# A two-block network on one core: one set of durations for the merge of threads, and a delta layer whose convolutions take their taps from PSUM

## The chip, the cores and the metric

One core of one Trainium2 chip runs the whole program in one launch. The time is the device time of that launch in microseconds (us); several runs are taken, and their median is the time of a kernel. TensorE does the matmuls (PE in the profile, its weight loads PEld), VectorE is DVE, ScalarE is ACT, GpSimd is POOL; SyncE (SP) issues the loads of weights. PSUM is the memory that matmuls write, SBUF the one that all other operands lie in.

## The reference, cut to what matters

Two blocks of a network in float32 on one sequence: 256 rows of width 1024, ahead of which the first block puts 16 rows of "meta" tokens (272 rows in the kernel). The first block has two layers: a gated delta layer and an mLSTM, each followed by a feed-forward part with a short convolution. The second block is a swiglu, three mixers side by side (spatial gating, latent attention, memory attention) under gates, and a second swiglu. The change touches the delta layer's projection and convolution:

```python
proj = h @ w_in
qkv = jax.nn.silu(causal_depthwise_conv(proj[..., :o1], conv_w)).astype(f32)
z = proj[..., o1:o2].astype(f32).reshape(B, L, GDN_V_HEADS, GDN_HEAD_DIM)
...
a_mat = jnp.eye(CHUNK, dtype=f32) + jnp.einsum('bhnid,bhnjd->bhnij', kb, kc) * decay * strict
rhs = jnp.concatenate([vc * bc[..., None], kb * jnp.exp(G)[..., None]], -1)
sol = lax.linalg.triangular_solve(a_mat, rhs, left_side=True, lower=True)
...
o = rms_norm(o, norm_w) * jax.nn.silu(z)
return o.reshape(B, L, GDN_VAL_DIM).astype(h.dtype) @ w_out
```

q and k have 1024 columns each, v and z 2048 each; the convolution has 4 taps along the rows for each of the 4096 columns of q, k and v.

## The kernel before, in words

**Products.** Activations lie with features on the partitions and the 272 rows along the free axis. A float32 product is made of three matmuls, since operands are split into a high part and the rest: `linear_g` (L398) runs for each of 8 blocks of 128 input features k, and for each feature tile of 128 output columns, wh x xh, wh x xl and wl x xh, all into one PSUM bank of the tile (`ps`). So a feature tile is 24 matmuls of 128x272. `wload` (L357) brings 512 KB of weights by one DMA on SP's queue (`wraw`), ACT copies them to `wh`, and wl = wraw - wh is formed by POOL in two pieces of 128x512 in the delta layer, elsewhere mostly by DVE. Buffers for wraw, wh and wl: three each.

**The delta layer** (20 to 368 us of the span; `gdn`, L1316). Several coroutines share the engines. `projections` runs `gdn_proj` for four groups of heads g (each 2 blocks of 256 columns of k and q and 2 of v, so 8 feature tiles) and puts the 8 blocks of z (`gdn_z`) wherever a group may not begin yet: group 2 begins when group 0's work ahead of the recurrence is done, group 3 after group 1's. `before`, in two lanes (first and second 128 rows), transposes and norms q and k (`kqp`, `kqT`), forms the decayed products (`kk`, `dp`, BA) and inverts the triangular matrix by blocks: level by level, a matmul `yp` (RT x Br), ACT's copy of it (Y), the matmuls `w`, and DVE's write of the new blocks into RT, which the next `yp` needs; `zp`, Z and `r2p` end it with a correction. A core coroutine runs the recurrence (`up`, `vs`, `sp`, `op`), `after` the norm of the output (`on`, `otp`, the root `rq_a`). The last 16 rows of all heads are a last small chunk, the tail (`gdn_tail_pre` and what follows it); `rsp`, `r`, `zs`, `og` lead from it to project_out (`ps<-og`, first at 368.32 us).

A block of the projection of q, k or v: two loads of 128x4x256 (four k each), for each load 12 matmuls on either feature tile, so that the two banks of the pool "pq" are both in use and end 12 matmuls apart. Then `conv4` (L974) for each: ACT copies PSUM to SBUF (`cx`), ACT scales PSUM by the last tap (`cy`), DVE adds the three other taps from cx, shifted by 1, 2 and 3 rows, ACT takes tanh of the half (`cth`), and DVE or (from feature tile 14 on, so all 16 of v and two of k) POOL makes the silu in one or two operations.

**What sets the order.** PE's order is written by `Threads` (L97 on, its loop `run`). Coroutines yield lists of what their next matmuls need: tiles, tags of banks or numbers. The planner keeps a clock for PE and lists of busy times for ACT, DVE and POOL ("A", "V", "G"), fills them by `COST` (a fixed part and one for each column), scaled by `KC`; `LAG`, `SAME` and `PLAG` are the handover from another engine, on the same engine, and to PE. It resumes the coroutine whose needs are met first. The order within DVE, ACT and POOL is made by the scheduler of the language from the program in that order. So another set of durations gives another order of the same matmuls.

Of the kernel before, what the change touches and what calls it, by code (L numbers as in the profile page):

```python
# [8 lines left out]
F32 = mybir.dt.float32  # L9
# [5 lines left out]
ALU = mybir.AluOpType  # L15
# [6 lines left out]
T = S + NM  # L22
KD = D // 128
# [73 lines left out]
class Threads:  # L97
# [4 lines left out]
    LAG, SAME, PLAG = 0.25, 0.13, 0.6  # L102
    KC = 1.0
    COST = {"PE": (0.0, 1 / 2400), "A": (0.06, 0.00085), "V": (0.07, 0.00104), "G": (0.1, 0.0022)}
# [29 lines left out]
    def note(self, key, outs, ins, n, ahead=False):  # L134
        a, b = self.COST[key]
        t = max([self.ready(x, key) for x in ins], default=0.0)
        if key == "PE":
            t = self.clk["PE"] = max(t, self.clk["PE"]) + a + b * n
        else:
            t = self.place(key, self.clk["PE"] if ahead else t, (a + b * n) * self.KC)  # L140
        for x in ins:
            self.read[x.tensor.name] = max(t, self.read.get(x.tensor.name, 0.0))
        for o in outs:
            self.rdy[o.tensor.name] = (0.0, key) if ahead else (t, key)
# [64 lines left out]
class Kern:  # L209
    def __init__(self, ctx, tc, ins, out):  # L210
# [20 lines left out]
        self.lane = None  # L231
        self.ordered = False
# [47 lines left out]
    def ps(self, shape=(128, T), name="ps"):  # L280
        return self.pp.tile(list(shape), F32, tag="pp", name=name)
# [536 lines left out]
    def embed(self):  # L818
# [3 lines left out]
        f = self.xt  # L822
# [3 lines left out]
        w = self.i["gdn_w_in"][0]  # L826
# [7 lines left out]
        with self.tc.manual_schedule(engines={mybir.EngineType.DVE}):  # L834
# [24 lines left out]
            low = {1: prefetch(0, KD, 6144, 32), 3: prefetch(0, 4, 1024, 256), 6: prefetch(4, 4, 1024, 256)}  # L859
# [114 lines left out]
    def conv4(self, ps, ct, out):  # L974
# [3 lines left out]
        x = self.p_l.tile([128, T], F32, tag="cx", name="cx", bufs=3)  # L978
        self.A.copy(x[:], ps)
        self.act(y[:], ps, AF.Copy, scale=w(3))  # L980
        for s in (1, 2, 3):
            self.stt(y[:, s:], x[:, :T - s], w(3 - s), y[:, s:], ALU.mult, ALU.add)
# [8 lines left out]
    def gdn_proj(self, X, g):  # L991
        W = self.i["gdn_w_in"][0]
        qs, ks, v0, v1 = (self.vslot() for _ in range(4))
        for base, dst in ((1024 + g * 256, ks), (g * 256, qs), (2048 + g * 512, v0), (2304 + g * 512, v1)):
            yield from self.linear_g(W, base, 256, KD, X, T, lambda m, p: self.conv4(p, base // 128 + m, dst[:, m, :]))
# [710 lines left out]
    def first(self):  # L1706

        i = self.i
        X = self.embed()
        self.th.KC, self.th.LAG, self.th.SAME, self.th.PLAG = 0.8, 0.25, 0.18, 0.65  # L1710
        Y = yield from self.gdn(X)
        self.th.KC, self.th.LAG, self.th.SAME, self.th.PLAG = 0.9, 0.25, 0.13, 0.6
# [68 lines left out]
        self.th.KC, self.th.LAG, self.th.SAME, self.th.PLAG = 0.9, 0.3, 0.13, 0.7  # L1781
# [666 lines left out]
```

## Time and profile before

| | us |
|---|---|
| median of 3 runs | 1668.43 |
| lowest and highest | 1667.3, 1671.02 |
| the profiled execution, its own time | 1671.11 |
| its span | 1669.3 |
| mean granted clock of TensorE | 0.973 |

The profile is of one execution. Rows of it are groups of instructions by line, engine, operation and tile (out<-in); since a helper records every operation, nearly all have line L190, and one goes by tiles. "Idle before" is time in which the engine did nothing ahead of these instructions, and what ended it. The chain of waits follows the end of the program (or of a stretch) back through what released each step. PE's records of matmuls overlap, so that a matmul's price is read from the distance of starts.

### The profile page before, as it was taken

Reading aid. Unit: us, or ns where it says so; the run is one execution under the profiler, and the core shown is the slowest. Engines: PE = TensorE matmul, PEld = TensorE weight load, DVE = VectorE, ACT = ScalarE, POOL = GpSimd, SP = SyncE. Lnnn points to the kernel's source line nnn. Section 1 sums busy time; section 2 is a strip of 40 time slices with the busy share of each in tenths; the row PEclk is TensorE's granted clock in tenths of the full one; section 3 lists DMA queues with packets and bytes.
Section 4 is the critical chain, followed back from the end, with each engine's and each line's share of the span. In section 5 each row is a group of like instructions: output and inputs, shape, how many; then the busy total and the mean of one; then the engine's idle time right before and its main releaser. Section 6 shows DMA issues by size and latency. Waiting matters only on the chain.

```text
span 1669.3 us, 31255 instructions
## 1 busy us (share of the span) xinstructions
PE 1564.4 (94%) x11980; PEld 1475.4 (88%) x11980; DVE 1120.0 (67%) x2223; ACT 927.9 (56%) x1877; POOL 579.2 (35%) x535
## 2 busy tenths in 40 slices
PE   8889888899999998999899998999997899999999
PEld 6788778799899997888899998999985789999987
DVE  5788877766888757457877668464659663566643
ACT  4567767655566554446566556454553655564542
POOL 3574555320200002550344441122275548511221
PEclk9799999999999999999999999999998999999999
DMA  5331221226355554335366564566553335656564
GB/s 158 89 89 52 69 64 47 77 90 214 106 178 174 169 175 111 96 115 164 107 185 192 175 185 148 163 199 192 173 166 111 111 93 150 183 164 188 180 189 151
DMA packets 239100, 235.39 MB, mean 141 GB/s; under 512 B 11511, under 2 KB 226407, under 8 KB 238951
## 3 DMA queue, kind: packets, MB, share of 16 engines
q1 hardware_dynamic: 238326, 231.86, 46.4%
q8 instruction: 94, 1.54, 0.4%
q0 software_dynamic: 496, 1.41, 0.4%
q14 instruction: 56, 0.45, 0.1%
q10 hardware_dynamic: 128, 0.13, 0.0%
HBM read 232.32 MB, written 1.05 MB: 140 GB/s over the span
## 4 chain that ended last, share of the span: by engine, by line
PE 68%; DVE 22%; ACT 5%; DMA 3%; issue 2%; POOL 0%; ACTq 0%; POOLq 0%; DVEq 0%
PE ps L190 52%; PE pst L190 5%; DVE cy L190 3%; DVE rq_a L190 3%; ACT wh L190 2%; DVE RT L190 2%; DVE wl L190 1%; DVE rq_y L190 1%; PE memp L190 1%; DMA wraw<-in_ffn_w_up_dram 1%; DVE xn L190 1%; PE rsp L190 1%; DVE on L190 1%; PE w L190 1%; PE up L190 1%
## 5 line engine op out<-in xcount | busy, mean ns | idle before, releaser
L190 PE MATMUL ps<-xhl,wh 128*128 128x256 f32 (+2 forms) x4496 | 861.6, 294 | 28.9 <-DVE py L190 11.1
L190 PEld LDWEIGHTS ps<-xhl,wh 128*128 128x128 f32 x4496 | 703.0, 193 | 38.3 <-DVE py L190 6.9
L190 ACT CAST wh<-wraw 128x1024 fp32r<-128x1024 f32 (+2 forms) x436 | 448.0, 1029 | 389.8 <-PE ps L190 255.9
L190 PE MATMUL ps<-xhl,wl 128*128 128x256 f32 (+2 forms) x2248 | 626.0, 287 | 0.8 <-DVE wl L190 0.8
L383 POOL TENSOR_TENSOR wl<-wraw,wh 128x512 fp32r<-128x512 f32 (+3 forms) x264 | 334.7, 1291 | 658.2 <-ACT wh L190 622.8
L190 PEld LDWEIGHTS ps<-xhl,wl 128*128 128x128 f32 x2248 | 423.9, 192 | 1.0 <-DVE wl L190 1.0
L190 DVE TENSOR_TENSOR wl<-wraw,wh 128x1024 fp32r<-128x1024 f32 (+2 forms) x237 | 287.4, 1213 | 182.4 <-ACT wh L190 179.2
L190 POOL TENSOR_TENSOR wl<-wraw,wh 128x512 fp32r<-128x512 f32 x134 | 173.9, 1319 | 153.1 <-ACT wh L190 136.2
L190 PE MATMUL ps<-hh,wh 128*128 128x256 f32 (+1 forms) x1056 | 191.1, 283 | 0.0
L190 PEld LDWEIGHTS ps<-hh,wh 128*128 128x128 f32 x1056 | 163.2, 189 | 0.0
L190 PE MATMUL ps<-hh,wl 128*128 128x256 f32 (+1 forms) x528 | 149.7, 284 | 0.0
L190 DVE SCALAR_TENSOR_TENSOR fy<-ps,pvt,fy 128x256 f32<-128x256 f32 (+2 forms) x176 | 84.9, 488 | 25.1 <-ACT fy L190 23.2
L190 PEld LDWEIGHTS ps<-hh,wl 128*128 128x128 f32 x528 | 99.4, 188 | 0.0
L190 DVE SCALAR_TENSOR_TENSOR cy<-cx,pvt,cy 128x271 f32<-128x271 f32 (+2 forms) x96 | 74.5, 779 | 13.5 <-ACT cy L190 12.5
L190 DVE TENSOR_TENSOR hh<-fy,hh 128x256 fp32r<-128x256 f32 (+1 forms) x88 | 64.4, 735 | 13.2 <-ACT hh L190 12.8
L190 POOL MEMSET mvt<- 128x4 f32 x4 | 0.4, 102 | 176.0 <-PE ps L190 176.0
L190 ACT ACTIVATE fy<-ps,pvt 128x272 f32<-128x272 f32 (+1 forms) x88 | 49.5, 568 | 12.3 <-PE ps L190 11.8
L190 DVE TENSOR_TENSOR py<-ps,rstd 128x256 f32<-128x256 f32 x72 | 29.9, 420 | 37.9 <-PE ps L190 37.9
L190 PE MATMUL pst<-wh,hh 128*128 128x512 f32 x176 | 55.1, 394 | 0.0
L190 ACT CAST hh<-fy 128x256 fp32r<-128x256 f32 (+1 forms) x88 | 35.7, 407 | 29.8 <-DVE fy L190 29.0
L190 DVE CAST_PREDICATED RT<-lvl,w 128x512 f16<-128x512 uint8 x67 | 44.9, 683 | 7.1 <-PE w L190 6.8
L190 PE MATMUL ps<-og,wh 128*128 128x272 f32 x256 | 48.6, 289 | 0.1
(523 smaller groups left out, 2420.4 us busy)
## 6 DMA issues: line engine op xcount, KB each, us to landing
wraw<-in_ffn_w_up_dram SPq DMA_DIRECT2D x88, 512.0 KB
wraw<-in_ffn_w_gu_dram SPq DMA_DIRECT2D x88, 512.0 KB
wraw<-in_ffn_w_down_dram SPq DMA_DIRECT2D x79, 512.0 KB
wraw<-in_gdn_w_in_dram SPq DMA_DIRECT2D x48, 512.0 KB
wraw<-in_w_in_dram SPq DMA_DIRECT2D x41, 512.0 KB
wraw<-in_ml_w_in_dram SPq DMA_DIRECT2D x24, 512.0 KB
wraw<-in_gdn_w_out_dram SPq DMA_DIRECT2D x16, 512.0 KB
wraw<-in_ml_w_out_dram SPq DMA_DIRECT2D x8, 512.0 KB
```

The source lines that it names most:

```text
L190: r = f(*args, **kw)
L383: eng.tensor_tensor(l[:, a, b], r[:, a, b], h[:, a, b].bitcast(F32), ALU.subtract)
```

## The change

Three things. The planner's durations become one set for the whole program, and `KC` goes; the settings that the delta layer, the stages after it and the mixers had are taken out. `conv4` loses the copy cx: the three taps read the PSUM bank itself. `gdn_proj` goes by feature tile: one load of 128x8x128 holds all eight k of one tile, a tile takes one bank, and before it starts the planner is told to wait for the last reader of the tile two back (`free`).

```diff
--- before.py
+++ after.py
@@ -99,9 +99,8 @@
 
 
 
-    LAG, SAME, PLAG = 0.25, 0.13, 0.6
-    KC = 1.0
-    COST = {"PE": (0.0, 1 / 2400), "A": (0.06, 0.00085), "V": (0.07, 0.00104), "G": (0.1, 0.0022)}
+    LAG, SAME, PLAG = 0.25, 0.05, 0.6
+    COST = {"PE": (0.006, 0.000441), "A": (0.19, 0.00084), "V": (0.155, 0.00104), "G": (0.1, 0.0025)}
 
     def __init__(self):
         self.clk = {"PE": 0.0}
@@ -137,7 +136,7 @@
         if key == "PE":
             t = self.clk["PE"] = max(t, self.clk["PE"]) + a + b * n
         else:
-            t = self.place(key, self.clk["PE"] if ahead else t, (a + b * n) * self.KC)
+            t = self.place(key, self.clk["PE"] if ahead else t, a + b * n)
         for x in ins:
             self.read[x.tensor.name] = max(t, self.read.get(x.tensor.name, 0.0))
         for o in outs:
@@ -229,6 +228,7 @@
         self.p_s = self.pool(ctx, "psm", 2)
         self.p_t = self.pool(ctx, "ptiny", 2)
         self.lane = None
+        self.taken = []
         self.ordered = False
         self.mixing = False
         self.near_load = self.seg = 0
@@ -278,7 +278,16 @@
         return t
 
     def ps(self, shape=(128, T), name="ps"):
-        return self.pp.tile(list(shape), F32, tag="pp", name=name)
+        t = self.pp.tile(list(shape), F32, tag="pp", name=name)
+        self.taken.append(t.tensor.name)
+        return t
+
+    def free(self, t):
+
+        n = self.taken.index(t.tensor.name)
+        key = f"pp{n % 2}"
+        self.th.bank[key] = self.taken[n - 2] if n > 1 else None
+        return key
 
     def pcore(self, shape=(128, 4, 128), name="pcs"):
         return self.pc.tile(list(shape), F32, tag="pc", name=name)
@@ -856,7 +865,7 @@
             for t, (o, P) in enumerate(TT):
                 self.ts(rd[:P, t, :P], self.ident[:P, :P], r[:P, t:t + 1], ALU.mult)
             self.columns(self.norms, 0)
-            low = {1: prefetch(0, KD, 6144, 32), 3: prefetch(0, 4, 1024, 256), 6: prefetch(4, 4, 1024, 256)}
+            low = {1: prefetch(0, KD, 6144, 32), 3: prefetch(0, KD, 1024, 128), 6: prefetch(0, KD, 1152, 128)}
             self.masks()
             for k in range(KD):
                 self.lane = k % 4
@@ -975,11 +984,9 @@
 
         w = lambda j: self.pv(PV_GC + j * 32 + ct)
         y = self.sm(name="cy")
-        x = self.p_l.tile([128, T], F32, tag="cx", name="cx", bufs=3)
-        self.A.copy(x[:], ps)
         self.act(y[:], ps, AF.Copy, scale=w(3))
         for s in (1, 2, 3):
-            self.stt(y[:, s:], x[:, :T - s], w(3 - s), y[:, s:], ALU.mult, ALU.add)
+            self.stt(y[:, s:], ps[:, :T - s], w(3 - s), y[:, s:], ALU.mult, ALU.add)
         th = self.sm(name="cth", tag="th")
         self.act(th[:], y[:], AF.Tanh, scale=0.5)
         if ct >= 14:
@@ -992,7 +999,11 @@
         W = self.i["gdn_w_in"][0]
         qs, ks, v0, v1 = (self.vslot() for _ in range(4))
         for base, dst in ((1024 + g * 256, ks), (g * 256, qs), (2048 + g * 512, v0), (2304 + g * 512, v1)):
-            yield from self.linear_g(W, base, 256, KD, X, T, lambda m, p: self.conv4(p, base // 128 + m, dst[:, m, :]))
+            for m in range(2):
+                ps = self.ps((128, T))
+                yield [self.free(ps)]
+                yield from self.linear_g(W, base + m * 128, 128, KD, X, T,
+                                         lambda _, p: self.conv4(p, base // 128 + m, dst[:, m, :]), [ps])
         tl = slice(256, T)
         self.G.tensor_copy(self.kqtail[:, 0, 2 * g:2 * g + 2, :], ks[:, :, tl])
         self.G.tensor_copy(self.kqtail[:, 1, 2 * g:2 * g + 2, :], qs[:, :, tl])
@@ -1707,9 +1718,7 @@
 
         i = self.i
         X = self.embed()
-        self.th.KC, self.th.LAG, self.th.SAME, self.th.PLAG = 0.8, 0.25, 0.18, 0.65
         Y = yield from self.gdn(X)
-        self.th.KC, self.th.LAG, self.th.SAME, self.th.PLAG = 0.9, 0.25, 0.13, 0.6
         self.ordered = True
         self.gctx.close()
         self.pb = self.pool(self.ctx, "pb", 1, space=PSUM)
@@ -1778,7 +1787,6 @@
         b1.close()
         self.p_c = None
         self.p_b2 = self.pool(self.ctx, "pb2", 1)
-        self.th.KC, self.th.LAG, self.th.SAME, self.th.PLAG = 0.9, 0.3, 0.13, 0.7
         yield from self.mixers(X)
         yield from self.last()
```

SP, which issues the loads of weights, from the vectors ahead of the delta layer to its end; before:

```order
L522 DMA vrow<-in_gdn_norm_w_dram 1x128
L367 DMA wraw<-in_gdn_w_in_dram 128x4x256 x4
L1523 DMA mgb<-in_ml_gate_b_dram 128x8
L367 DMA wraw<-in_gdn_w_in_dram 128x4x256 x40
L367 DMA wraw<-in_gdn_w_out_dram 128x4x256 x6
```

and after:

```order
L531 DMA vrow<-in_gdn_norm_w_dram 1x128
L376 DMA wraw<-in_gdn_w_in_dram 128x8x128 x4
L1534 DMA mgb<-in_ml_gate_b_dram 128x8
L376 DMA wraw<-in_gdn_w_in_dram 128x8x128 x16
L376 DMA wraw<-in_gdn_w_in_dram 128x4x256 x2
L376 DMA wraw<-in_gdn_w_in_dram 128x8x128 x8
L376 DMA wraw<-in_gdn_w_in_dram 128x4x256 x14
L376 DMA wraw<-in_gdn_w_out_dram 128x4x256 x6
```

The loads of q, k and v have the new form (128x8x128), and group 3's eight stand behind the first block of z (128x4x256, two loads) instead of ahead of all z.

DVE at the first convolutions (cy), among the gates' logarithm (lp); before:

```order
L190 TENSOR_SCALAR lp<-lp 128x96
L190 RECIPROCAL lp<-lp 128x96
L190 SCALAR_TENSOR_TENSOR cy<-cx,pvt,cy 128x271
L190 TENSOR_TENSOR lp<-lp 128x96
L190 SCALAR_TENSOR_TENSOR cy<-cx,pvt,cy 128x270
L190 TENSOR_TENSOR lp<-lp 128x96
L190 SCALAR_TENSOR_TENSOR cy<-cx,pvt,cy 128x269
```

and after:

```order
L189 SCALAR_TENSOR_TENSOR cy<-ps,pvt,cy 128x271
L189 TENSOR_SCALAR lp<-lp 128x96
L189 SCALAR_TENSOR_TENSOR cy<-ps,pvt,cy 128x270
L189 RECIPROCAL lp<-lp 128x96
L189 SCALAR_TENSOR_TENSOR cy<-ps,pvt,cy 128x269
L189 TENSOR_TENSOR lp<-lp 128x96 x2
L189 SCALAR_TENSOR_TENSOR cy<-ps,pvt,cy 128x271
```

The taps read ps, and the first stand two operations further ahead.

PE at the end of the delta layer, around the last chunk's recurrence; z is `ps<-xhl`; before:

```order
L190 MATMUL up<-R_5070,bv 128x128 x2
L190 MATMUL up<-wq,St 128x2x16 x16
L190 MATMUL otp<-eye,on 128x128 x2
L190 MATMUL ps<-xhl,wh 128x272 x2
L190 MATMUL ps<-xhl,wl 128x272
L190 MATMUL ps<-xhl,wh 128x272 x2
L190 MATMUL ps<-xhl,wl 128x272
L190 MATMUL ps<-xhl,wh 128x272 x2
L190 MATMUL ps<-xhl,wl 128x272
L190 MATMUL vnp<-eye,vnT 128x128 x2
```

and after:

```order
L189 MATMUL up<-R_5177,bv 128x128 x2
L189 MATMUL up<-wq,St 128x2x16 x16
L189 MATMUL otp<-eye,on 128x128 x2
L189 MATMUL vnp<-eye,vnT 128x128 x2
L189 MATMUL otp<-eye,on 128x128 x2
L189 MATMUL up<-BA,vn 128x128 x2
L189 MATMUL rsp<-sq,ones 128x256
L189 MATMUL ps<-og,wh 128x272 x2
L189 MATMUL ps<-og,wl 128x272
```

Of z, nothing is left at this place; its last matmuls have moved ahead of the last levels of the inverse.

## Rows read from the trace of the kernel before

**Rows 1.** The page, busy time of each engine: us, share of the span, instructions.

```profile
PE 1564.4 (94%) x11980; PEld 1475.4 (88%) x11980; DVE 1120.0 (67%) x2223; ACT 927.9 (56%) x1877; POOL 579.2 (35%) x535
```

**Rows 2.** Stages: length, busy us of PE, PEld, DVE, ACT, POOL; PEclk, DMA share, GB/s.

```profile
20.00:368.00 348.00, 300.65 (x2446) 274.22 (x2447) 265.28 (x631) 221.32 (x663) 181.14 (x196) 0.93 0.26 75
...
640.00:770.00 130.00, 120.40 (x859) 106.40 (x858) 74.92 (x192) 63.60 (x143) 55.01 (x46) 0.97 0.37 103
...
1220.00:1400.00 180.00, 160.01 (x1127) 145.85 (x1127) 121.19 (x352) 94.94 (x207) 103.23 (x84) 0.95 0.41 117
```

**Rows 3.** Table by 20 us inside the delta layer, the same columns.

```profile
60.00:80.00 20.00, 16.18 (x119) 14.71 (x118) 18.39 (x33) 11.00 (x35) 17.80 (x17) 0.96 0.46 129
...
220.00:240.00 20.00, 15.47 (x139) 14.28 (x137) 19.58 (x46) 11.84 (x32) 9.62 (x11) 0.97 0.38 106
```

**Rows 4.** Chain of waits, 0 to 368 us: shares by line.

```profile
by line: PE ps L190 18.0%; DVE cy L190 12.6%; DVE RT L190 7.1%; DVE rq_a L190 5.4%; DVE on L190 3.2%; PE w L190 3.0%; PE up L190 3.0%; PE warm L190 2.8%; issue 2.8%; PE dp L190 2.7%; DVE rq_y L190 2.4%; PE yp L190 2.1%; PE kk L190 2.0%; PE 
```

**Rows 5.** PE's waits, 20 to 368 us: total, times, longest.

```profile
PE yp L190 <- DVE RT L190: 13.7, 10, 3.3
...
PE zp L190 <- DVE RT L190: 4.8, 5, 2.2
```

**Rows 6.** Page, costliest groups; tile cy, ns min/median/max; a line, 20 to 360 us.

```profile
L190 DVE SCALAR_TENSOR_TENSOR cy<-cx,pvt,cy 128x271 f32<-128x271 f32 (+2 forms) x96 | 74.5, 779 | 13.5 <-ACT cy L190 12.5
...
L190 DVE SCALAR_TENSOR_TENSOR cy<-cx,pvt,cy x96: 476/512/1583, 33.8 to 257.6; 128x271 f32<-128x271 f32 x32, 128x270 f32<-128x270 f32 x32, 128x269 f32<-128x269 f32 x32
L190 ACT ACTIVATE cy<-ps,pvt x32: 484/494/558, 32.5 to 253.6; 128x272 f32<-128x272 f32 x32
...
L190 ACT COPY cx<-ps 128x272 f32<-128x272 f32 x32 | 12.4, 389 | 2.8 <-PE ps L190 2.7
```

**Rows 7.** Timeline of DVE: start, us, operation, count, idle before.

```profile
59.34 6.88 DVE L190 SCALAR_TENSOR_TENSOR cy<-cx,pvt,cy 128x271 f32<-128x271 f32 x6 [2.46 <-ACT cy L190]
```

**Rows 8.** Tile fy, 770 to 1220 us, ns min/median/max; a line, 450 to 700 us.

```profile
L190 DVE TENSOR_TENSOR fy<-fy,sg x22: 416/564/1504, 821.6 to 940.9; 128x256 f32<-128x256 f32 x22
L190 DVE TENSOR_TENSOR fy<-ps,sg x22: 409/422/425, 1032.9 to 1154.7; 128x256 f32<-128x256 f32 x22
...
L190 DVE SCALAR_TENSOR_TENSOR fy<-ps,pvt,fy 128x271 f32<-128x271 f32 x40 | 19.8, 495 | 0.0
```

**Rows 9.** Tile cy, 20 to 360 us: what it waited for, who waited for it.

```profile
  ACT cy L190: 12.5, 9
...
  PE ps L190: 1.4, 3
```

**Rows 10.** Lines of 20 to 360 us: busy, mean ns, idle before.

```profile
L190 POOL TENSOR_TENSOR wl<-wraw,wh 128x512 fp32r<-128x512 f32 x92 | 120.8, 1334 | 96.0 <-ACT wh L190 87.7 <-PE w L190 7.1 <-PE otp L190 1.2
...
L190 DVE CAST_PREDICATED RT<-lvl,w 128x512 f16<-128x512 uint8 x67 | 44.9, 683 | 7.1 <-PE w L190 6.8
L190 ACT ACTIVATE Y<-yp 128x256 f16<-128x256 f32 x99 | 36.2, 388 | 18.7 <-PE yp L190 18.5
...
L190 POOL TENSOR_TENSOR cth<-cth,cy 128x272 f32<-128x272 f32 x18 | 15.0, 832 | 29.2 <-ACT cth L190 29.2
```

**Rows 11.** Timeline of PE at the delta layer's end.

```profile
352.86 3.66 PE L190 MATMUL up<-wq,St 128*128 128x32 f32 x32
...
361.10 0.60 PE L190 MATMUL rsp<-sq,ones 128*128 128x256 f32 x2
...
368.32 0.56 PE L190 MATMUL ps<-og,wh 128*128 128x272 f32 x2
```

**Rows 12.** The same, within project_out.

```profile
370.34 0.41 PE L190 MATMUL ps<-og,wh 128*128 128x272 f32 x2
...
370.71 0.41 PE L190 MATMUL ps<-og,wh 128*128 128x272 f32 x2
```

**Rows 13.** PE's waits: 640 to 770 us (first row) and 1220 to 1400 us.

```profile
PE mbp L190 <- DVE mlf L190: 4.3, 1, 4.3
...
PE ps L190 <- DVE py L190: 6.3, 1, 6.3
```

## The prediction

> **What bounds the kernel now.** I read the page's busy shares first, then the table by stages, then inside the stage that the change touches the table by 20 us, the chain of waits and PE's waits. PE is busy for 94% of the span [rows 1]: over most of the program the time is TensorE's own, and only a stage in which PE waits has anything to give. Three have [rows 2]. The delta layer (20 to 368 us) leaves PE idle for 348.0 - 300.7 = 47 us, the mLSTM (640 to 770) for 9.6, the mixers (1220 to 1400) for 20. In the feed-forward stages between them PE is busy for 97% or more; the change moves nearly nothing there and I give them 0.
>
> In the delta layer no engine is full on average (DVE 265 of 348), but it has stretches in which DVE is: 18.4 of 20 us at 60 to 80 and 19.6 of 20 at 220 to 240, while PE falls to about 16 [rows 3]. The chain of waits up to the end of this stage says the same: 12.6% of it, 46 us of 368, are the convolutions' taps (DVE cy), more than any other DVE work [rows 4]. PE's longest waits there are for DVE too, for RT, a step of the blockwise inverse: 13.7 us before yp and 4.8 before zp [rows 5].
>
> **Part 1: taps read PSUM.** There are 96 taps of 269 to 271 columns, mean 779 ns [rows 6]. Their spread tells more: least 476, median 512, most 1583 [rows 6]. Six in a row took 6.88 us at 59 us [rows 7], 1147 each, while POOL was busy for 17.8 of 20 us [rows 3]. Two operations of one size in the feed-forward stages, where POOL also works, part by operand: with both tensors in SBUF (fy<-fy,sg) 416 to 1504 ns, with one in PSUM (fy<-ps,sg) 409 to 425, over 22 each [rows 8]. So a tap is stretched when both its tensors lie in SBUF and POOL is at work, and one that reads PSUM isn't. The very operation that the new tap becomes is there already: fy<-ps,pvt,fy at 271 columns, mean 495 [rows 8]. [...]
>
> Saving: 96 x (779 - 495) = 27 us of DVE time. What of it lies on the path: the chain's 46 us of taps would be 46 x 495/779 = 29, so 17 us less, if nothing else steps in. Bounds: none (all hidden) to 27. I take 15, a little under the chain's figure, since POOL and PE stand close behind.
>
> **Part 2: the cx copies go.** 32 copies of 389 ns [rows 6], 12.4 us of ACT, which is busy for 221 of 348 us [rows 2]. They stood ahead of cy on ACT, and DVE waited 12.5 us for cy, in 9 places [rows 9]; each such wait shortens by at most 0.39. That is 3.5 us of DVE idle time; I take 2, bounds 0 and 3.5.
>
> **Part 3: 128-column blocks.** Matmuls, their operands and the 32 loads of 512 KB stay in number and size; a load's runs become 512 bytes in place of 1 KB, and the splits wh (ACT) and wl (POOL) are the same. DMA is at 0.26 of its engines in this stage and 0.46 in the fullest 20 us shown [rows 2, 3]; even if a load took twice as long, the share would stay below 1, so 0. Loads of group 3 now stand on SP's queue after one z block (its order stands with the change); they are issued as buffers come free, far ahead of use: 0.
>
> What does change is how long a PSUM bank is held. Two banks are used in turn. A feature tile is 24 matmuls, 0.126 us each (three every 0.375 [rows 12]): 3.0 us. Before, two tiles of a block ended 1.5 us apart and a bank was free after two ACT operations, 0.39 + 0.50 [rows 6]. Now it is free after ACT's cy and three taps: 0.50 + 3 x 0.50 = 2.0 us, out of 3.0 until PE needs it. 1.0 us is left for handovers and for what stands ahead on DVE. PE's waits for banks were 1.4 us in all [rows 9]; the planner now counts them (the tag that gdn_proj yields). I take 0, bounds -1 and the first rival's price.
>
> **Part 4: the planner's durations.** They move PE's order, not what is computed. With 0.126 us for each ps matmul and the like for others, I counted the PE work that stands between a step of the inverse and the step that needs its result. Before the last z block, the quarter with the least cover rises from 1.49 to 1.58 us (yp) and from 1.32 to 1.46 (w), the median from 1.80 to 1.97 and 1.47 to 1.86. A level needs about 0.39 for Y and 0.68 for RT [rows 10] besides its matmuls and handovers, some 2 us in all. The waits for RT (18.5 us [rows 5]) are those that more cover shortens, but Part 1 takes from the same waits. I take 4, bounds 0 and 9.
>
> The price stands at the end of the stage. Before, z matmuls fill PE right up to project_out; now the last z matmul comes some 16 us of PE work earlier, and behind it stand 29 steps of the inverse with less than about 1 us of other PE work between them and what they wait for, where there were 4 in the whole stage. Worked out: five levels of some 2 us (10), zp to R 1.7, up and its way to rsp 7 (8.2 in the trace, z matmuls between; 3.7 of it the run of 32 small matmuls), and rsp to the first og matmul, which took 368.32 - 361.10 = 7.2 [rows 11]: 26 us. Before, the last 16 us of PE work of this stage took 22, from 346 to 368 by the same count. So +4; with waits that don't lie as evenly as that sum has them, up to +8. I take +6.
>
> In the mLSTM and the mixers the order moves a little: the matmuls that wait now (mbp 4.3, ps for py 6.3 [rows 13]) come one to three us of PE work later or stay. I take -1 and -2; bounds: nothing of it, or +5, and -8 (the half of what the two stages lose to waits).
>
> **Sum.** -15 - 2 - 4 + 6 - 1 - 2 = -18 us. Against the profiled execution (1671.11 us, its span 1669.3) this is 1653; that execution lies 2.7 above the median of the three runs, 1668.43, and against the median it is 1650.5. This kernel's runs tell about 0.2%, some 3.3 us, from no change.
>
> **Rivals.**
> A, slower: the banks. The taps stand in DVE's queue among the lanes' work, and DVE is full in stretches. If they wait 2 us on average in place of at most 1.0, PE stands 1 us at each of 32 tiles, +32 - 18: 1682. It decides from 18/32 = 0.6 us beyond the 1.0 on. For it: DVE at 19.6 of 20 us [rows 3]. Against it: that fullness is itself the long taps, and between a lane's tiles lies other PE work. 15%.
> B, smaller: POOL takes over. It forms wl in two pieces of 1.33 and for 18 of the 32 tiles cth and kv, 0.83 and about as much [rows 10]: 4.3 us a tile against PE's 3.0. Where POOL is full (60 to 80, 17.8 [rows 3]) shorter taps win nothing. Half of Part 1 and of Part 2 then go: 1659. Against it: POOL is full only there, 181 of 348 in the stage [rows 2]. 20%.
> C, no change: one set of durations suits the mixers and the mLSTM less than their own did, and the uncovered inverse at the end costs more than I took: +5 and +8 on top of a body that gives 13 and not 21: 1668. 10%.
> D, the taps are no cheaper: if a PSUM operand cost DVE more each time than the copy's source, Part 1 falls and 1665 is left. Rows speak against it: 495 from PSUM, 512 the median from SBUF, 476 the least [rows 6, 8]. 5%. [...]
>
> **How the numbers follow.** Forecast 50%, 1640 to 1660; B 20%, D 5%, C 10%, A 15%. Faster by over 0.2% (below 1665.1): all of the forecast, most of B, half of D, a fifth of C: 0.72. Slower (above 1671.8): A and four tenths of C: 0.18. The rest 0.10. The range 1634 to 1676 leaves out most of A and a sliver of the forecast below.
>
> **What would show it.** Right: taps at about 495 ns with no spread; DVE's busy time 25 to 29 us lower and ACT's 12; the chain's cy share near 8% of its first part; the waits of yp and zp for RT below 12 us before 340 us; og starting near 352 to 357. The tail: after the last z matmul, waits of 6 to 10 us on yp, w and r2p that were not there. Wrong: waits of ps for DVE cy (banks) of more than 10 us; POOL above 18 of 20 in several windows with DVE idle for it; or the stage shorter by 15 and the mixers longer by 5.

## The result, and the profile after

The changed kernel takes 1706.26 us (median of 4 runs, 1704.09 to 1708.29), the kernel before 1667.87 (4 runs): ratio 1.022, 95% interval 1.0201 to 1.024. It is slower by some 38 us; the prediction was 18 faster. Its profiled execution has a span of 1703.5 us, 34.2 more than before, and that is what the rows below divide.

The page of the kernel after, busy times and the group of the taps:

```profile
PE 1580.0 (93%) x11980; PEld 1488.3 (87%) x11980; DVE 1096.0 (64%) x2223; ACT 921.5 (54%) x1845; POOL 573.5 (34%) x535
...
L189 DVE SCALAR_TENSOR_TENSOR cy<-ps,pvt,cy 128x271 f32<-128x271 f32 (+2 forms) x96 | 47.3, 493 | 24.8 <-ACT cy L189 23.7
```

The taps did what was said of them: 493 ns each, 27 us of DVE time gone from the group [rows 6], 24 from the engine [rows 1]. Yet the table by stages (length, busy us of PE, PEld, DVE, ACT, POOL; PEclk, DMA share, GB/s) has the delta layer 24 us longer:

```profile
20.00:392.00 372.00, 308.15 (x2450) 279.57 (x2449) 242.09 (x640) 219.07 (x639) 174.59 (x196) 0.90 0.26 73
...
340.00:360.00 20.00, 13.72 (x96) 10.80 (x96) 11.19 (x38) 10.42 (x40) 1.48 (x3) 0.83 0.00 1
360.00:380.00 20.00, 13.18 (x80) 10.85 (x81) 11.14 (x43) 5.71 (x22) 0.00 (x0) 0.81 0.00 1
380.00:392.00 12.00, 7.64 (x29) 5.61 (x28) 3.58 (x13) 7.09 (x15) 0.00 (x0) 0.50 0.00 1
```

DVE is busy for 242 us there (265 before [rows 2]). What stands out are the last 50 us: PE is busy two thirds of the time, and from 380 on its granted clock is 0.50. Over the whole stage PE is busy 7.5 us longer for the same matmuls (308.15 against 300.65 [rows 2]) at a mean granted clock of 0.90 against 0.93; so an estimate from these two rows puts some 7.5 of the 24 us down to the lower clock and the other 16.5 to more idle time of PE. The timeline of PE at that end, after:

```profile
331.43 0.28 PE L189 MATMUL ps<-xhl,wl 128*128 128x272 f32 x1
...
343.37 0.39 PE L189 MATMUL kqp<-eye,kqtail 128*128 128x128 f32 x2
...
376.36 6.87 PE L189 MATMUL up<-wq,St 128*128 128x32 f32 x32
...
387.08 1.22 PE L189 MATMUL rsp<-sq,ones 128*128 128x256 f32 x2 [0.80 <-ACT sq L189]
...
391.64 1.12 PE L189 MATMUL ps<-og,wh 128*128 128x272 f32 x2 [3.33 <-ACT og L189]
```

The first row is the last z matmul. The 32 small matmuls take 6.87 us where they took 3.66, the first pair of project_out 1.12 where it took 0.56, and rsp stands 26 us later than before [rows 11]. The tail's first step, kqp of kqtail, is at 343.37; in the timeline before it was

```profile
304.93 0.39 PE L190 MATMUL kqp<-eye,kqtail 128*128 128x128 f32 x2
```

So the lanes arrive at the tail 38 us late. Of these, 15 are made up by project_out (391.64, before 368.32), since no z lies between any more. PE's waits up to there, after:

```profile
PE kqp L189 <- ACT kqtok L189: 24.9, 8, 6.8
PE gp L189 <- DVE gg L189: 6.9, 1, 6.9
PE ps L189 <- DVE cy L189: 5.3, 6, 1.6
PE otp L189 <- DVE on L189: 5.1, 2, 2.9
PE yp L189 <- DVE RT L189: 4.1, 8, 1.6
```

yp's waits for RT did fall, from 13.7 to 4.1 us [rows 5]; another has grown, kqp behind kqtok (the transposes of the normed q and k, behind the root that DVE makes in small operations). Before, it was

```profile
PE kqp L190 <- ACT kqtok L190: 6.7, 4, 3.5
```

Of the 34.2 us, 23.3 arise ahead of project_out, 3.2 from there to the mLSTM, 6.2 in the mLSTM and 4.3 in the mixers; 2.9 are won between these two. The 3.2 lie at the start of project_out, which now follows a stretch of waits. Its first microseconds, before and then after, have a granted clock of 1.00 and 0.76:

```profile
368.00:378.00 10.00, 10.00 (x81) 9.90 (x81) 9.66 (x22) 8.64 (x18) 0.00 (x0) 1.00 0.37 116
```

```profile
391.00:402.00 11.00, 10.36 (x65) 10.13 (x66) 6.94 (x25) 5.85 (x13) 0.00 (x0) 0.76 0.47 154
```

### The profile page after: what moved, and what is told of

It is laid out like the page before. It is cut to its first block, busy times and chain, and to the rows that moved or that the text cites. A ratio compares the mean times of both kernels' runs of the same rounds, so it can differ in the third digit from the quotient of the medians.

```text
span 1703.5 us, 31236 instructions
## 1 busy us (share of the span) xinstructions
PE 1580.0 (93%) x11980; PEld 1488.3 (87%) x11980; DVE 1096.0 (64%) x2223; ACT 921.5 (54%) x1845; POOL 573.5 (34%) x535
## 4 chain that ended last, share of the span: by engine, by line
PE 69%; DVE 14%; ACT 5%; issue 2%; DMA 1%; POOL 0%; ACTq 0%; DVEq 0%; POOLq 0%
PE ps L189 54%; PE pst L189 4%; DVE rq_a L189 2%; ACT wh L189 1%; DVE rq_y L189 1%; PE memp L189 1%; DVE wl L189 1%; PE up L189 1%; PE rsp L189 1%; PE w L189 1%; DVE xhl L189 1%; DVE RT L189 1%; PE mnp L189 1%; DVE xn L189 1%; PE ksp L189 0%
## 5 line engine op out<-in xcount | busy, mean ns | idle before, releaser
L189 DVE TENSOR_TENSOR hh<-fy,hh 128x256 fp32r<-128x256 f32 (+1 forms) x88 | 64.0, 730 | 13.6 <-ACT hh L189 13.4
L189 DVE SCALAR_TENSOR_TENSOR cy<-ps,pvt,cy 128x271 f32<-128x271 f32 (+2 forms) x96 | 47.3, 493 | 24.8 <-ACT cy L189 23.7
L189 ACT ACTIVATE fy<-ps,pvt 128x272 f32<-128x272 f32 (+1 forms) x88 | 49.6, 568 | 13.2 <-PE ps L189 12.8
L189 DVE CAST_PREDICATED RT<-lvl,w 128x512 f16<-128x512 uint8 x67 | 45.5, 685 | 15.2 <-PE w L189 14.2
```

Of the source, the lines that this page charges most:

```text
L189: r = f(*args, **kw)
```

## Experiments

18 kernels were run. The table has what is compared again and again: the ratio to the kernel before, and for the profiled execution the start of the tail's first kqp and of project_out, and two of PE's waits in the delta layer (kqp for kqtok, ps for DVE cy). These four columns and every span below are of one execution each, and executions of one kernel lie apart: those of e16 run from 1661.21 to 1678.0 us. PE's order behind project_out is the same, matmul for matmul, in before and in the 15 kernels with the old settings there, and yet that part took 1297.4 us (e1) to 1309.4 (e13). So a difference of a few microseconds between two spans says little.

| kernel | median us | ratio (95%) | tail's kqp at | project_out at | kqtok | cy |
|---|---|---|---|---|---|---|
| before | 1668 | 1 | 304.9 | 368.3 | 6.7 | 0 |
| the change | 1706.26 | 1.022 (1.0201 to 1.024) | 343.4 | 391.6 | 24.9 | 5.3 |
| e1 old durations | 1670.67 | 1.0001 (0.9989 to 1.0012) | 305.8 | 367.6 | 8.8 | 2.9 |
| e2 new durations alone | 1715.82 | 1.0282 (1.025 to 1.0314) | 352.2 | 400.3 | 6.3 | 0 |
| e3 taps alone | 1680.67 | 1.0085 (1.0059 to 1.0111) | 303.8 | 369.7 | 1.1 | 16.4 |
| e4 z held | 1707.21 | 1.0231 (1.021 to 1.0251) | 341.0 | 393.7 | 24.7 | 4.5 |
| e5 new durations in the delta layer | 1692.87 | 1.0149 (1.0125 to 1.0173) | 343.8 | 392.1 | 25.2 | 6.8 |
| e6 the same at 0.8 | 1686.25 | 1.0112 (1.0089 to 1.0134) | 313.9 | 378.8 | 21.2 | 2.4 |
| e7 blocks with cx | 1698.15 | 1.0171 (1.0149 to 1.0193) | 332.6 | 393.1 | 17.6 | 0 |
| e8 the same at 0.7 | 1677.64 | 1.0055 (1.004 to 1.007) | 294.0 | 373.9 | 8.7 | 1.4 |
| e9 before's order, taps from PSUM | 1672.77 | 1.002 (1.0 to 1.004) | 300.9 | 366.1 | 2.4 | 21.1 |
| e10 e1's order, with cx | 1689.69 | 1.012 (1.0086 to 1.0153) | 322.2 | 383.9 | 12.6 | 0 |
| e11 the change's order, with cx | 1723.51 | 1.0325 (1.0282 to 1.0369) | 362.7 | 410.7 | 29.3 | 0 |
| e12 ACT's duration alone | 1682.27 | 1.0077 (1.0048 to 1.0106) | 316.1 | 373.7 | 12.6 | 1.6 |
| e13 old, no wait for banks in the plan | 1671.28 | 1.0014 (1.0002 to 1.0026) | 301.5 | 362.1 | 6.4 | 3.9 |
| e14 old, unscaled | 1685.15 | 1.0106 (1.0085 to 1.0126) | 334.3 | 383.7 | 20.4 | 2.8 |
| e15 new, old handovers | 1684.67 | 1.0103 (1.0081 to 1.0125) | 330.0 | 376.0 | 13.0 | 5.6 |
| e16 old, LAG 0.15 | 1671.56 | 1.0008 (0.9986 to 1.0031) | 294.4 | 367.1 | 5.1 | 2.5 |
| e17 new, SAME 0.18 | 1696.47 | 1.018 (1.0106 to 1.0254) | 340.3 | 391.4 | 15.2 | 5.2 |
| e18 old, SAME 0.05 | 1670.85 | 1.0004 (0.997 to 1.0038) | 296.7 | 367.8 | 17.8 | 0.4 |

### Which part of the change: e1 to e4

e1 is the change with the planner as it was:

```diff
-    LAG, SAME, PLAG = 0.25, 0.05, 0.6
-    COST = {"PE": (0.006, 0.000441), "A": (0.19, 0.00084), "V": (0.155, 0.00104), "G": (0.1, 0.0025)}
+    LAG, SAME, PLAG = 0.25, 0.13, 0.6
+    KC = 1.0
+    COST = {"PE": (0.0, 1 / 2400), "A": (0.06, 0.00085), "V": (0.07, 0.00104), "G": (0.1, 0.0022)}
...
+        self.th.KC, self.th.LAG, self.th.SAME, self.th.PLAG = 0.8, 0.25, 0.18, 0.65
         Y = yield from self.gdn(X)
+        self.th.KC, self.th.LAG, self.th.SAME, self.th.PLAG = 0.9, 0.25, 0.13, 0.6
```

(and the mixers' line). 

> The change with the planner's old durations and its old settings per stage; taps from PSUM and the blocks of one feature tile stay. Theory 1 (filler): the new durations make the planner see the lanes' steps as not ready, put z matmuls in their place, and so the lanes come late and the end of the delta layer runs bare. Then this kernel keeps the gain of the taps: project_out starts at 350 to 362 us, the whole at 1648 to 1662. Theory 2 (banks): taps on DVE hold the PSUM banks and the new blocks make PE and the lanes wait; the durations are harmless. Then project_out still starts later than 380 and the whole is over 1690.

Level with before, and in neither theory's range: the durations carry the whole loss, but the expected gain of the taps is not there either, though DVE is 20 us and ACT 4 us less busy up to project_out, as the stage's row of e1 shows beside [rows 2]:

```profile
20.00:368.00 348.00, 299.24 (x2451) 274.55 (x2452) 245.07 (x642) 216.90 (x642) 175.42 (x196) 0.93 0.27 75
```

e2 is the opposite, the kernel before with the new `COST`, `SAME` and without `KC` and the three settings. 

> The kernel before with the new durations alone; the copy cx and the 256-column blocks stay. Theory 1: z runs out even earlier in PE's order (at 219 us of PE work out of 253, where the change has 236), so project_out starts later than 390 and the whole is 1705 to 1730. Theory 2: no bank is held by taps, so project_out starts at 360 to 370 and the whole is 1655 to 1675.

Theory 1 holds: without any tap from PSUM the durations alone make project_out 32 us late.

e3 takes the taps alone, in blocks of 256 columns:

```diff
-        x = self.p_l.tile([128, T], F32, tag="cx", name="cx", bufs=3)
-        self.A.copy(x[:], ps)
...
-            self.stt(y[:, s:], x[:, :T - s], w(3 - s), y[:, s:], ALU.mult, ALU.add)
+            self.stt(y[:, s:], ps[:, :T - s], w(3 - s), y[:, s:], ALU.mult, ALU.add)
```

> The kernel before with the taps read from PSUM and without cx; blocks of 256 columns and the old durations stay. Two tiles of a block end 1.5 us apart and a bank is held for some 2.3. Theory 1: the shorter taps gain 10 to 15 us, bank waits give back 3 to 8: 1653 to 1668. Theory 2: the held banks decide, PE's waits for DVE cy are over 20 us, and the whole is over 1675.

The time is theory 2's, and PE's waits for banks, 16.4 us, are near the 20 that it names (1.1 us of kqtok waits are left). So theory 2 has its place, but with the old blocks: those of the change have 2.9 in e1. The trace is of the fastest of e3's four executions and has project_out only 1.4 us late; where the rest of the 11 us of its median lies is not shown.

e4 holds back the last z blocks of the change:

```diff
                     if nz == 6:
-                        yield from pre_done[2]
+                        yield from pre_done[3]
+                    if nz == 7:
+                        yield tail_pre
```

> The change with the last two blocks of z held back in the merge: the seventh until both lanes have done the work ahead of the recurrence of group 3, the eighth until the tail's preparation is done. Theory 1: 12 us of z matmuls cover part of the bare end; project_out starts 5 to 14 us earlier than in the change (378 to 387), the whole is 1692 to 1702. Theory 2: the end is not what costs; within 3 us of the change, 1703 to 1709.

A miss of my theory in this form; the time is theory 2's. The last z matmul moved from 331 to 368 us and project_out came no earlier (393.7). The bare end is a consequence: behind the tail's first kqp stands a chain that filling does not shorten. What counts, as I read it, is when that chain begins.

### Sizes of durations, and the blocks: e5 to e8

e5 sets the new `COST`, `KC` 1.0 and SAME 0.05 ahead of `gdn` and the old ones behind it. 

> The change with the new durations in the delta layer alone; from the first feed-forward part on the planner has its old durations and settings again. If the durations cost in each stage by themselves, the delta layer stays at the change's time (project_out starts at 390 to 393 us), and what the change lost after it (about 6 us in the mLSTM, 5 in the mixers, 1 to 2 at the first feed-forward part) comes back: 1693 to 1699. If the late end of the delta layer drags the later stages along, it stays at 1703 or more.

As expected, within a microsecond: project_out at 392.1 as in the change, and 10.7 us of span come back behind it (1703.5 - 1692.8). That is two single executions; over all traces the part behind project_out took 1309.9 to 1313.6 us in the four kernels with the new durations there (the change, e2, e4, e11; mean 1311.7) and 1297.4 to 1309.4 in the other 16 (mean 1303.8), so some 8. The mLSTM is the clearest piece of it: 124.8 to 125.0 us in those four, 118.7 to 122.0 in the others. Its waits of PE in the change, of which mdp and mnp were not there before:

```profile
PE mbp L189 <- DVE mlf L189: 2.8, 1, 2.8
PE mdp L189 <- DVE mwd L189: 2.3, 1, 2.3
PE mnp L189 <- ACT mjunk L189: 2.2, 1, 2.2
```

Others have gone (mbp was 4.3 [rows 13]), so waits explain only a part. The rows of the mLSTM, before and then after, have PE busy for 4.3 us more with the same 804 matmuls, at a clock of 0.95 against 0.97:

```profile
643.00:762.00 119.00, 111.10 (x804) 98.87 (x803) 65.56 (x173) 55.88 (x125) 55.01 (x46) 0.97 0.38 108
```

```profile
670.00:795.00 125.00, 115.40 (x804) 102.05 (x802) 65.78 (x172) 55.55 (x124) 55.47 (x46) 0.95 0.36 103
```

e6 and e8 scale the new durations in the delta layer (`KC` 0.8 and 0.7). 

> As the kernel before this one, but in the delta layer the new durations of ACT, DVE and POOL are all taken at 0.8. In PE's order the tail's first step then stands at 214 us of PE work (240 in the change, 207 before) and z lasts to the end. Theory 1 (the planner thinks the lanes later than they are, and puts z ahead of them): the delta layer is at most as long as with the old durations, project_out starts at 352 to 367, the whole is 1648 to 1668. Theory 3 (the set is bad by its proportions, a fixed part too large against the part for each column): project_out starts later than 375.

> As the run with the durations at 0.8, at 0.7: the tail's first step at 203 us of PE work, z left over behind the last step of the lanes (10 us or more). Theory 1: PE now waits for the lanes in the body, more than at 0.8, while z stays for the end: project_out 2 to 10 us later than at 0.8, 1655 to 1675. Theory 3: again later than 375.

Smaller durations bring the lanes forward (tail's kqp at 343.8, 313.9, 294.0) and the time down, but not to the old settings: e6 missed theory 1's range for project_out by 12 us and fulfils theory 3's words (378.8, later than 375); e8 is in neither theory's range for project_out: expected to be later than e6, it is 5 us earlier, and with its lanes 11 us ahead of before its stage is still 6 us longer. So lateness is not all of it, and the set's proportions are not ruled out.

e7 is e1 with the copy and the taps from SBUF (the two lines of e3 put back). 

> The old durations and the blocks of one feature tile, with the copy cx and its taps kept: 25 us of DVE and 12 of ACT more than the run with the old durations. If DVE and ACT do not set PE's waits in that order (the taps gain nothing because PE's order is the bound), within 3 us of it: 1664 to 1672. If the taps gain and the new blocks give the same back, 10 to 17 us over it: 1678 to 1688.

Over both ranges, 33.7 us of span over e1 (1698.7 against 1665.0; 27.5 by the medians, since e1's trace is of its fastest execution and e7's of its slowest). But the planner saw the copy and made another order, so this mixes two things.

### The order held fixed: e9 to e12

The next three keep PE's order instruction for instruction and change only what DVE and ACT do. In e9 (from the kernel before) the planner is told of a copy that isn't issued:

```diff
-        x = self.p_l.tile([128, T], F32, tag="cx", name="cx", bufs=3)
-        self.A.copy(x[:], ps)
+        x = Name(f"cx_{ct}")
+        self.th.note("A", [x], [ps], T)
...
-            self.stt(y[:, s:], x[:, :T - s], w(3 - s), y[:, s:], ALU.mult, ALU.add)
+            self.nc.vector.scalar_tensor_tensor(y[:, s:], ps[:, :T - s], w(3 - s), y[:, s:], ALU.mult, ALU.add)
+            self.th.note("V", [y[:, s:]], [x, w(3 - s), y[:, s:]], T - s)
```

> The kernel before with its PE order kept instruction for instruction (the planner is told of the old copy and the old taps), but the copy is not issued and the taps read PSUM. So this is Parts 1 and 2 alone. If the prediction's 17 us for the shorter taps and the missing copies hold, project_out starts at 350 to 360 us and the whole is 1650 to 1660, less what the banks take (blocks of 256 columns: up to 10). If PE's order, not DVE, sets the waits, project_out stays at 365 to 371.

e10 and e11 do the reverse in e1 and in the change: copy and taps from SBUF, `note` tells the planner of taps from ps. 

> The run with the old durations and the new blocks, its PE order kept instruction for instruction, with copy and taps from SBUF put back behind the planner's back: 25 us of DVE and 12 of ACT more. If the shorter taps are worth 17 us in a fixed order, it is 12 to 25 us slower than that run (1677 to 1695). If nothing, within 3 us (1664 to 1673). The run that let the planner see the copy was 29 us slower; if most of that was its other PE order, this one is near the lower end.

> The same for the change: its PE order kept, copy and taps from SBUF put back. In the change the lanes run late and are the bound, so DVE counts at least as much as elsewhere: 12 to 30 us slower than the change (1716 to 1737) if the taps are worth 17 us; within 3 us (1702 to 1711) if PE's order is all.

These settle the taps. e10 and e11 came as the first theory of each had it: in e1's order the shorter taps and the missing copy are worth 383.9 - 367.6 = 16.3 us up to project_out, in the change's 410.7 - 391.6 = 19.1. e9 did not: project_out at 366.1 is in the second expectation's range, and its 1672.77 us lie beyond the first's, even with 10 us for the banks. The rows of the stage, e10 and then e11, have DVE at 275 us in place of 245 and 242:

```profile
20.00:384.00 364.00, 302.63 (x2449) 277.58 (x2450) 275.17 (x642) 226.08 (x673) 182.76 (x196) 0.92 0.26 71
```

```profile
20.00:411.00 391.00, 312.05 (x2449) 282.21 (x2449) 275.02 (x640) 227.52 (x670) 184.45 (x196) 0.90 0.25 69
```

And in before's own order, with its blocks of two tiles, the gain turns into the wait that rival A named. PE's waits of e9:

```profile
PE ps L196 <- DVE cy L988: 21.1, 12, 5.1
PE yp L196 <- DVE RT L196: 7.5, 8, 1.6
PE ps L196 <- DVE zs L196: 4.6, 2, 4.0
PE zp L196 <- DVE RT L196: 4.5, 4, 2.3
```

yp's waits fell by 6 and kqtok's by 4, and 21.1 us of waits for banks stand against it. So it isn't PE's order alone that sets the waits, as e9's second expectation has it: the wait has moved from RT to the banks. The blocks of one tile take these waits away (2.9 in e1), but with taps from SBUF they have a cost: e10, which has them and the old taps in an order planned for taps from PSUM, is 17.7 us of span over before (1687.0 against 1669.3), and e7, in an order of its own, 29.4. With taps from PSUM they are worth 10 us instead (e3 1680.67, e1 1670.67).

e12 is e1 with `"A": (0.19, 0.00084)` in the delta layer and nothing else. 

> The run with the old durations, in whose delta layer ACT alone has its new duration (0.19 + 0.00084 for a column in place of 0.06 + 0.00085, at 0.8). In PE's order the tail's first step stands at 228 us of PE work (207 with the old, 241 in the change). Theory 1: the lanes come late in proportion, project_out starts at 373 to 386 and the whole is 1672 to 1690. If ACT's part does not matter, 366 to 370 and 1664 to 1673.

Theory 1's, with project_out at the lower edge of its range: one engine's duration alone, made longer, moves the tail's kqp 10 us and project_out 6 us back.

### Handovers, scale, and the plan's wait for banks: e13 to e18

e13 takes `yield [self.free(ps)]` out of e1. 

> The run with the old durations, without the line that makes the planner wait for a PSUM bank (PE itself still waits). If the planner's wait costs the taps' gain, project_out starts 3 to 12 us earlier than in that run (355 to 365 us against 367.6), the whole is 1655 to 1664. If banks must be planned for, PE's waits of ps for DVE cy rise from 2.9 to over 8 us and the whole is 1668 to 1680.

Project_out starts 5.5 us earlier, as the first expectation has it; but the whole, 1671.28, is not faster. Behind project_out e13's trace takes 1671.5 - 362.1 = 1309.4 us where e1's takes 1297.4, though PE's order is the same there in both. e13's is the slowest of its ten executions and e1's the fastest of its ten, so these 12 us can't be put down to the kernels. Some 3 of them lie at the start of project_out, where e13 has PE waiting ahead of it (ps for ACT's og, 2.4 us). Whether the line costs anything is therefore not shown.

e14 takes the old durations in the delta layer at 1.0 in place of 0.8, e15 the new ones with SAME 0.18 and PLAG 0.65. 

> The run with the old durations, in the delta layer taken at 1.0 in place of 0.8. In PE's order the tail's first step moves from 207 to 239 us of PE work, as in the change (241). Theory 1 (size alone): project_out starts at 382 to 395, the whole is 1680 to 1697. If it is the new set's proportions, it stays within 6 us of the old: 366 to 374.

> The run with the new durations in the delta layer alone, with the handovers that the stage had before (SAME 0.18, PLAG 0.65). If the short handover made the root too early in PE's order, the waits of kqp for kqtok fall from 25 us to under 12 and project_out starts before 384 (392.1 with the short one). Theory 1: lateness is as before (the tail's first step at 240 us of PE work), project_out at 388 to 397.

e14 is theory 1's: the very durations that the kernel was level with, 1.25 times as long, cost 16 us up to project_out. e15 is a miss of it, 12 us below its range, with the kqtok waits halved. e17 and e18 then change SAME alone, e16 LAG alone. 

> The run with the new durations in the delta layer alone, with SAME at 0.18 in place of 0.05 and nothing else. If the short handover between operations of one engine is what puts the second kqp too early, its waits for kqtok are 10 to 16 us (25.2 and, with both handovers old, 13.0) and project_out starts at 373 to 381. If PLAG did it, the waits stay over 20 and project_out is at 387 to 395.

> The run with the old durations, in the delta layer with SAME at 0.05 in place of 0.18. If SAME costs by itself, PE's waits of kqp for kqtok rise from 8.8 to over 15 us and project_out starts at 374 to 385 (367.6). If it costs only together with the long durations, the waits stay under 12 and project_out is at 364 to 372.

> The run with the old durations, in the delta layer with the handover between engines at 0.15 in place of 0.25: the lanes stand still a little earlier in PE's order (first otp at 113 us of PE work against 116). If earlier lanes help further, project_out at 358 to 366 and the whole 1655 to 1664; if the old settings stand at the best point, PE waits more for RT and it is 368 to 376, 1666 to 1676.

SAME does rule the kqtok waits, both ways (8.8 to 17.8 from e1 to e18, 25.2 to 15.2 from e5 to e17); the first lines of PE's waits of e18 and e17:

```profile
PE kqp L190 <- ACT kqtok L190: 17.8, 4, 5.6
PE gp L190 <- DVE gg L190: 8.0, 1, 8.0
```

```profile
PE kqp L190 <- ACT kqtok L190: 15.2, 6, 5.1
PE gp L190 <- DVE gg L190: 6.2, 1, 6.2
```

But those waits do not rule the time: e18 has 17.8 us of them and is level with before, e17 has 15.2 and starts project_out at 391.4. Its two executions are 9.6 us apart (1701.26 and 1691.69), so part of e15's gain may be such scatter. e15 and e17 differ in PLAG alone (0.65 and 0.6), and project_out is 15 us apart; how PLAG would do that stays open. e16 is level. None of the 18 beats the kernel before.

## Why the prediction was wrong

Adding up the spans from kernel to kernel: before 1669.3; the new blocks, in an order made for them, +17.7 (e10); taps from PSUM and no copy -22.0 (e1); the new durations in the delta layer +27.8 (e5); the same durations behind it +10.7 (the change, 1703.5). By the medians the four steps are +21.6, -19.0, +22.2 and +13.4. The prediction had them at 0, -17, +2 and -3. How the first two share is a matter of the way through the kernels, since the blocks gain or lose with the taps; that together they are level with before is shown by e1.

**Parts 1 and 2 held.** The reading of the tap's spread (two SBUF operands against POOL: 476 to 1583 ns before [rows 6], 391 to 501 with taps from PSUM in the change), its new price (495 said, 493 found) and its worth on the path (15 and 2 said, 16.3 and 19.1 in two fixed orders) were right for blocks of one tile. In before's own order, with blocks of two, the waits for banks took it back (e9).

**Part 3 lacked a term.** The banks were rightly put at little for the new blocks (5.3 us of waits in the change) and DMA at nothing (its share of the stage is 0.26 before and after). But the blocks were put at 0 because matmuls, operands and loads stay, and that left out that blocks of one tile give the planner another order to make. With the old taps that order costs 18 to 29 us (e10, e7), about what the taps gain, and so e1 is level. What in the order costs it was not found; the plan's wait for banks may be 5.5 us of it up to project_out (e13), which is within the scatter.

**Part 4, the price of the durations' order, is the step that failed.** It put the delta layer at -4 for more cover between the lanes' steps and their needs and +6 for the end without z, +2 in sum. From e1 to e5, which differ in the delta layer's durations and handovers alone, project_out moves by 392.06 - 367.63 = 24.4 us. The tail's first kqp in e1, then in e5:

```profile
305.82 0.38 PE L190 MATMUL kqp<-eye,kqtail 128*128 128x128 f32 x2
```

```profile
343.79 0.39 PE L190 MATMUL kqp<-eye,kqtail 128*128 128x128 f32 x2
```

The reading of the cover was right as far as it went: PE's waits of yp for RT fell from 12.1 (e1) to 3.7 (e5), though only with the shorter taps (13.5 in e2, 12.8 in e11). But cover in PE's order is z and projections put ahead of the lanes, and the lanes pay. The table shows both sides. Where the tail's first kqp comes by 306 us (before, e1, e3, e8, e9, e13, e16, e18), project_out starts between 362 and 374: z lasts until it is reached or nearly, and PE's own work and waits set the end. Where it comes at 330 or later with at most 3 us of z matmuls behind it (e2, e5, e11, e14, e15, e17 and the change), project_out follows 46 to 51 us behind it, whatever came before: 343.4 to 391.6 in the change. That is the chain of the tail, bare, with nothing to fill PE's waits, and in the change at a granted clock of 0.83, 0.81 and 0.50 (340 to 360, 360 to 380 and 380 to 392 us). The other five (e4, e6, e7, e10, e12) have 6 to 31 us of z behind the tail's kqp, and project_out 53 to 65 us behind it. The chain from kqp over the root, the decayed products, the inverse, the recurrence and rsp was visible before, at 63 us with z between; I began its count with five levels of the inverse behind the last z matmul, and so wrote 26 us from there to project_out where the change took 391.6 - 331.7 = 60. PE's order, read at the tail's first kqp instead of at the last z, says it: 207 us of PE work before, 241 after, of 253 (the count that the expectations of e2 and e12 use). So 12 us of PE work were left for a chain of 48. The granted clock of such an end (0.50 from 380 to 392 us in the change, and in e4) was in no term either.

That longer durations put the lanes later, and project_out with them, is shown by e2, e5, e12 and e14. That project_out is late because the lanes are is read from the seven traces above; no run moved the lanes alone. That it isn't the only thing is shown too: e8 and e16 bring the lanes 10 us ahead of before and gain nothing, and e6 and e10 are 10 and 16 us late at project_out although z lasts to the end or nearly. There PE has lost the time in the body, in e6 with 21 us of kqtok waits. Why the waits for kqtok grow with the durations as well as with SAME (20.4 in e14) stays open.

**The later stages** were put at -3 and cost 10.7 in the two spans, some 8 over all traces. The rival that spoke of this (C, one set suits them less, and a bare end) had part of the mechanism and a third of the size: +5 and +8 against 10.7 and 27.8. Rival A's wait for banks shows in the blocks of before (16.4 in e3, 21.1 in e9) and hardly in those of the change (5.3).

None of the prediction's signs of being wrong came, and some of those of being right did (the taps, the waits for RT); the one that told was og at 391.6 and not at 352 to 357. ACT's busy time fell by 6.4 us in place of 12. Two figures of the prediction are slightly off, and nothing hangs on them: the second feed-forward stretch (770 to 1220 us) has PE busy for 434.5 of 450 us, 96.5%, and 1668.43 - 18 is 1650.4.

## What to carry to other kernels

When a planner places filler between the steps of a long dependent chain, more cover per step is not a gain by itself: find the first step of the last chain in the old and the new order and ask how late it now stands, then add the bare length of that chain. Durations in such a planner are priorities as well as times; here the longer ones (ACT's 128x256 at 0.405 us where the old set had 0.222; the trace has 0.388 for Y [rows 10]) gave the worse order, though this one is the nearer to the trace. And to price one edit in a kernel whose order is planned, keep the order fixed as in e9 to e11; with the planner free, the same copy cost 33.7 us of span (e7) where it cost 22.0 (e10).

## What the runs showed of the hardware

A DVE operation of four columns took 4.72 us. The timeline of DVE in the change, and of POOL at the same time:

```profile
115.45 4.72 DVE L189 TENSOR_SCALAR rq_y<-rq_v 128x4 int32<-128x4 int32 x1
120.20 0.16 DVE L189 SCALAR_TENSOR_TENSOR rq_a<-rq_y 128x4 f32<-128x4 f32 x1
```

```profile
115.44 0.76 POOL L189 TENSOR_TENSOR kv<-cth,cy 128x272 f32<-128x272 f32 x1
116.17 0.76 POOL L189 TENSOR_TENSOR cth<-cth,cy 128x272 f32<-128x272 f32 x1
116.89 2.53 POOL L189 TENSOR_TENSOR wl<-wraw,wh 128x512 fp32r<-128x512 f32 x2
119.39 0.76 POOL L189 TENSOR_TENSOR kv<-cth,cy 128x272 f32<-128x272 f32 x1
```

It reads one SBUF tensor and ended as POOL's fifth operation in a row did (119.39 + 0.76 = 120.15); the nine operations of its kind (rq_y<-rq_v) in the delta layer have a median of 0.17 us. The longest wait of kqp in the change (6.8 us) ends behind it. The prediction's reading, that a tap is stretched when both its tensors lie in SBUF and POOL is at work, doesn't cover an operation with one. That this one waited for POOL is my reading of the two timelines; no run shows it apart.

The other eight of its kind took 0.16 to 1.26 us in the same kernel, and what sets this one apart from them is not shown. Before, where the taps read SBUF, no operation of the roots up to project_out took over 1.3. And the roots did not grow longer as a whole: their 163 operations took 51.5 us together in the change and 50.8 before.
